# A hybrid decoder layer on one core: first head's logits one k tile later, its key sums seven k tiles apart, and the second chunk's first block loaded in the first down pair

## The chip, the cores and the metric

The kernel runs on 1 core of one Trainium2 chip. The metric is the device time of one execution in microseconds. The core has a matrix engine (TensorE, shown as PE, with its weight loads as PEld), a vector engine (DVE), a scalar engine (ACT), GpSimd (POOL), which here computes a little and issues DMAs, and SyncE (SP), which here only issues DMAs. All DMAs, whichever engine issues them, run on the core's 16 DMA engines.

## The reference

One decoder layer over 528 tokens (16 learned meta tokens and 512 tokens of input) with 2048 channels, all in float32:

```python
n = _rmsnorm(h, g_mix[l])
p = n @ w_in[l]                      # columns: q, k, v | b, c, u
o_attn = ...  # 8 heads of 128: z = q.k/sqrt(128) after RMS norm of q and k per head,
              # A[t,s] = sigmoid(z) * prod_{s<j<t} (1 - sigmoid(z_tj)), strictly causal
o_conv = gb * _causal_dwconv(gc * u, conv_w[l])          # 1024 channels, 3 taps
o = jnp.concatenate([_rmsnorm(o_attn, g_attn_out[l]), _rmsnorm(o_conv, g_conv_out[l])], axis=-1)
h = h + o @ w_out[l]
n2 = _rmsnorm(h, g_ffn[l])
h = h + (jax.nn.silu(n2 @ w_gate[l]) * (n2 @ w_up[l])) @ w_down[l]     # 5632 channels inside
```

The product over j is taken as a sum of logarithms over the keys behind s. The meta positions are dropped from the output.

## The kernel before

Everything is kept transposed: channels on the 128 partitions, tokens along the free axis. A float32 product is made of three matmuls: each operand is split into a high part (a cast to the matrix engine's fp32r type, on ACT) and a low part (the rest, a subtraction on DVE), and high x high, high x low and low x high are accumulated in PSUM. So each weight tile costs a DMA by SP into `w_buf` (L172), a cast on ACT into `s_buf` (L188) and a subtraction on DVE (L189). `split` (L293 to L295) does the same for activations.

The stages, in order of time:

- **Heads** (to about 338 us). For each of 8 heads the products k, q and v over 16 k tiles of 128 channels (`product`, L280 to L284, some 0.72 us a k tile). Attention work of a head is hung into the products of the next one: `after(n, work)` (L260) puts work on a list, and every k tile calls `tick` (L263), which runs what has come due. `attend` (L508) transposes v and makes the logits z (L527 to L533), `sums(2)`, `sums(1)`, `sums(0)` (L577) sum over the keys by matmuls with a triangle of ones into tiles c (L582 to L588), and `mix` (L607) makes the head's output o. For the first head, `attend` is due 11 k tiles after v, `sums(2)` 14 later, the other sums 6 apart and `mix` 11 later; for the others `attend` is due after 6.
- **Short convolution** (to about 595 us), two channel tiles by plain products, the other six by pairs of tiles, in `pair_product` (below).
- **Output projection** (to about 770 us). For each of 16 tiles i an attention half (`oa`) and a conv half (`oc`) of `wide_product` (L848 to L850) go into one PSUM tile `po` of two banks, `po[:, 0]` and `po[:, 1]`. For the last two tiles both attention halves come first, then both conv halves. DVE scales the halves in L907 and L931.
- **Gate and up** (to about 1610 us): 44 pairs f of `pair_product`, which makes a two by two block product of weights and activations with seven block products in place of eight. It has PSUM banks x, y, z; the order is block 0 into x, 1 into z, 2 onto x, 3 onto z, 4 onto x, 5 into y, 6 onto x (in the first pair of a weight matrix block 5 comes first). Between them ACT copies x and z aside (L769, L772, and after block 2 the copy u2, L775), and DVE makes c2 (L778 behind block 3, L783 behind block 4) and c1 (L788). `gate` (L1049) then makes silu(gate) * up; for odd f it makes five mixed blocks `odd` and `store_acts` splits them (L294 on ACT, 1280 wide, L295 on DVE) and stores them to DRAM tiles `fd` through POOL (L1043).
- **Down** (to the end). The 5632 channels are four chunks of 4, 6, 6 and 6 k tiles in pairs. For a chunk c the seven activation blocks (c, 0) to (c, 6) are loaded from `fd` by `load_acts` (L1067), two DMAs each on POOL (L1081). The first chunk has four pairs j of double width, which use `ring[0]` and the tiles `first1` to `first6`; the others have eight pairs each. Chunk 1 and later use twelve places of a ring in turn; block (1, 0) has place 6, block (1, 6) place 0. With `behind` given, POOL first makes a small write into the place (L1074) that reads a result of the pair before, which holds the load back until then. Results are scaled on DVE (L1121, L1127, L1128) and added to `out` by accumulating DMAs on POOL (L1113). The last pair adds on DVE instead and stores through SP (L1170 to L1177).

Memory places are taken from pools on two stacks; a new pool's tile waits for the last use of the tiles that lay there before. On the left stack, at the start of the down stage, `d` (8192 bytes a partition) and behind it ring place 6 (12544) come to lie where `f4` (16640) and the pool of `gu` (4864) lay.

The order of the instructions on each engine isn't that of the text: a planner simulates the program and picks, for each engine, the ready instruction with the best priority, which is the place in the text unless `tc.high_priority` raises it. `tc.stamp_issue_order_token(inst, name)` makes instructions of the same name keep the order of the text. Each engine, and POOL and SP as issuers of DMAs, then runs its instructions strictly in the order planned.

Of the kernel before, what the change touches and what calls it, by code (L numbers as in the profile page):

```python
# [12 lines left out]
ALU = mybir.AluOpType  # L13
# [9 lines left out]
KT = D // P  # L23
# [3 lines left out]
T2 = SEQ // 2  # L27
# [6 lines left out]
def hybrid_layer(ctx: ExitStack, tc: tile.TileContext, xT, w_in, w_out, w_gu, w_down, vecs, out):  # L34
# [148 lines left out]
    def split_quad(src, n, turn=False):  # L183
# [5 lines left out]
        in_turn(ve.tensor_tensor(lo, src, hi.bitcast(F32), ALU.subtract), turn)  # L189
        split_w.append((hi, lo, n))  # L190

    def in_turn(inst, on=True):
        if on:
            tc.stamp_issue_order_token(inst.ins, "first_pairs")
# [95 lines left out]
        for _ in product_steps(parts, acts, len(acts)):  # L290
            pass

    def split(hi, lo, src, eng=ve):  # L293
        sc.copy(hi, src)  # L294
        eng.tensor_tensor(lo, src, hi.bitcast(F32), ALU.subtract)  # L295

    def rsqrt(dst, v, n, y=None, t=None, eng=ve):
# [182 lines left out]
    def head(h):  # L480

        if h:
            pk = pp.tile([P, 2, 512], F32, tag="pp", name=f"pk{h}")
            product([(pk[:, 0, :H], 0, H), (pk[:, 1, :H], H, L)], n_hl)
        else:
            pk = pk0
        kn = kns[0]
        kh = apool.tile([P, 384], F32R, tag="kh", name=f"kh{h}")
        kl = apool.tile([P, 384], F32R, tag="kl", name=f"kl{h}")
        after(8 if h else 11, qk_norm(halves(pk, H), g_k, L, kn[:, :L], (kh, kl, 384), f"k{h}"))  # L490

        if h:
            pq = pp.tile([P, 2, 512], F32, tag="pp", name=f"pq{h}")
            product([(pq[:, 0, :], META, L)], n_hl)
        else:
            pq = pq0
        qn = apool.tile([P, SEQ], F32, tag="qn", name=f"qn{h}")
        qh = apool.tile([P, SEQ], F32R, tag="qh", name=f"qh{h}")
        ql = apool.tile([P, SEQ], F32R, tag="ql", name=f"ql{h}")
        after(9 if h else 12, qk_norm(pq[:, 0, :], gq_s, SEQ, qn, (qh, ql, SEQ), f"q{h}"))  # L500

        pv = pp.tile([P, 2, 512], F32, tag="pp", name=f"pv{h}")
        product([(pv[:, 0, :H], 0, H), (pv[:, 1, :H], H, L)], n_hl)
        vt = t512(L, "e", 2)
        ve.tensor_tensor(two(vt[:, :L]), halves(pv, H), two(r), ALU.mult)
        after(6 if h else 11, lambda: attend(h, kn, kh, kl, qn, qh, ql, vt))

    def attend(h, kn, kh, kl, qn, qh, ql, vt):  # L508

# [67 lines left out]
        def sums(s):  # L577
# [11 lines left out]
            if s:  # L589

                n, (a0, b0) = SEQ - Q0[s], SEG[s - 1]
                th, tl = hl[s - 1]
                ve.tensor_tensor(lw[0:1, b0 - n : b0], c[0:1, :n], sp[0:1, a : a + n], ALU.add)
                split(th[0:1, :], tl[0:1, :], lw[0:1, a0:b0])
                after(6, lambda: sums(s - 1))
            ve.tensor_tensor(lb[:, a:b], lb[:, a:b], c[:, : b - a], ALU.subtract)
            sc.activation(lw[:, a:b], lb[:, a:b], AF.Exp)
            causal(lw, s)
# [147 lines left out]
    def pair_product(acts, c1, c2, sides, m=1, fourth=None, second=None):  # L746
# [25 lines left out]
            sc.copy(p5, z)  # L772
        block_product(x, acts[2], False, m)
        with tc.high_priority(1 << 20):
            sc.copy(u2, x)  # L775
        block_product(z, acts[3], False, m)
        with tc.high_priority(1 << 20):
            in_turn(ve.scalar_tensor_tensor(c2[:, 0], z, -1.0, u2, ALU.mult, ALU.subtract), i == conv_pairs)  # L778
# [132 lines left out]
    for i, j in enumerate(OUT_TILES):  # L911
# [5 lines left out]
        if i < KT - 2:  # L917
            hj = attention_half(i, gp if half else ve)
        elif i == KT - 2:
            hs = [attention_half(m, ve) for m in (i, i + 1)]  # L920
        if i >= KT - 2:
            hj = hs[i - KT]
            run(wide_product(ps_out[i][:, 1, :], oc))
        ps = ps_out[i]
        t2 = wide_tmp("t2")
        if half == 1:

            src = hbuf.tile([P, 8, T2], F32, tag="src", name=f"src{k}")

        def residual(eng):  # L930
            ve.tensor_tensor(t2, ps[:, 1, :], acc_c, ALU.mult)  # L931
            eng.tensor_tensor(hj, hj, t2, ALU.add)
            sc.activation(src[:, 2 * half : 2 * half + 2], two(hj), AF.Copy, scale=g_ffn[:, j : j + 1])

# [98 lines left out]
    fd = [[dram.tile([P, 2, n, T2], F32R, name=f"fd{c}_{s}") for s in range(7)] for c, n in enumerate(CHUNKS)]  # L1033
    at = [(c, k) for c, n in enumerate(CHUNKS) for k in range(n)]

    def store_acts(blks, n, slots, kp):

        t = apool.tile([P, 2, n, T2], F32R, tag=f"s{n}", name=f"s{kp}_{n}")
        split(t[:, 0], t[:, 1], blks)
        c, k = at[kp]  # L1040
        for i, s in enumerate(slots):
            if kp < FT // 2 - 1:
                gp.dma_start(fd[c][s][:, :, k], t[:, :, i])  # L1043
            else:
                nc.sync.dma_start(fd[c][s][:, :, k].bitcast(F32), t[:, :, i].bitcast(F32))
# [3 lines left out]
    def gate(f, g1, u1, x):  # L1049
# [8 lines left out]
        else:  # L1058
# [3 lines left out]
            ve.tensor_tensor(odd[:, 2], odd[:, 1], even_f[:, 2], ALU.subtract)  # L1062
            ve.scalar_tensor_tensor(odd[:, 3], odd[:, 2], -1.0, even_f[:, 0], ALU.mult, ALU.subtract)
            ve.scalar_tensor_tensor(odd[:, 4], odd[:, 3], -1.0, odd[:, 0], ALU.mult, ALU.subtract)
            store_acts(odd, 5, (5, 6, 1, 2, 3), f // 2)

    def load_acts(c, s, behind=None):  # L1067

# [60 lines left out]
            add_down(j + n, c1[:, :, at])  # L1129

    for j in range(KT // 4):
        for s in ((0, 1), (2, 3), (4, 5))[j - 1] if j else ():
            load_acts(1, s, last)
        c1, c2 = (d, d2)[j % 2][:, 0:2], (d, d2)[j % 2][:, 2:4]
        last = c2[:, 0]
        x = pair_product(
# [11 lines left out]
    for c in range(1, len(CHUNKS)):  # L1148
        end = c == len(CHUNKS) - 1
        for j in range(KT // 2):  # L1150
# [18 lines left out]
            if last_pair:  # L1169
                ve.tensor_tensor(c2, c2, r_h, ALU.mult)  # L1170
                ve.tensor_tensor(c2, c2, h2[1], ALU.add)
                nc.sync.dma_start(two(out[2 * j + 1]), c2)
                ve.tensor_tensor(c1[:, 0], c1[:, 0], r_h[:, 0], ALU.mult)
                ve.tensor_tensor(c1[:, 0], c1[:, 0], h2[0][:, 0], ALU.add)
                ve.tensor_tensor(c1[:, 1], x, r_h[:, 1], ALU.mult)  # L1175
                ve.tensor_tensor(c1[:, 1], c1[:, 1], h2[0][:, 1], ALU.add)  # L1176
                nc.sync.dma_start(two(out[2 * j]), c1)  # L1177
            else:
                first_sums(2 * j, c1, x, 1)
    rings_p[2].release()  # L1180
# [61 lines left out]
```

## Time and profile before

| | us |
|---|---|
| median of 3 runs (lowest to highest) | 2040.29 (2039.11 to 2042.28) |
| the profiled execution's own time | 2040.52 |
| its span, first to last instruction | 2038.8 |
| PE busy | 2028.3 |
| DVE busy | 1721.0 |
| ACT busy | 1049.4 |
| POOL busy | 381.2 |

The span is that of one execution. Ends of matmuls are modelled, since matmuls are pipelined; the starts are measured, so the distance between starts tells what a matmul cost. In a row of a timeline stand the start, the length to the end of the last one, the engine, the line, the operation, what is written and read, and how many instructions the row holds; in brackets the engine's idle time ahead of it and who ended that.

### The profile page before, as it was taken

The numbers are of one execution on the slowest core, as the hardware profiler recorded it, in microseconds if no ns is written. First come the engines' busy times: TensorE is split into PE (matmuls) and PEld (weight loads), VectorE is DVE, ScalarE is ACT, GpSimd is POOL, SyncE is SP. The second block draws the span as 40 slices with busy tenths as digits, with TensorE's granted clock in tenths as the row PEclk, the third lists the DMA queues.
The fourth block names the chain that finished last, engine by engine and source line by source line (L and its number), as shares of the span: only waits on it lengthen the run. The fifth ranks groups of instructions, "written<-read, shape, count | busy, mean of one in ns | idle before, by whom it ended". The sixth has DMA issues, their size and how long they took to land.

```text
span 2038.8 us, 39740 instructions
## 1 busy us (share of the span) xinstructions
PE 2028.3 (99%) x16158; PEld 1966.2 (96%) x16158; DVE 1721.0 (84%) x2202; ACT 1049.4 (51%) x1517; POOL 381.2 (19%) x532
## 2 busy tenths in 40 slices
PE   9999999999999999999999999999999999999999
PEld 8999999999998889999999999999999999999999
DVE  8788878588977779989989989989989888888887
ACT  7666666344444436455555555555555544444443
POOL 0111111210015440111110110110110252222111
PEclk9999999999999999999999999999999999999999
DMA  6333344753366566555655654554655999989864
GB/s 231 113 117 125 125 137 130 254 146 104 104 219 184 177 189 224 166 163 169 169 162 149 170 164 146 171 161 150 167 161 151 289 305 292 247 236 260 231 152 89
DMA packets 161863, 361.70 MB, mean 177 GB/s; under 512 B 13584, under 2 KB 73488, under 8 KB 161680
## 3 DMA queue, kind: packets, MB, share of 16 engines
q1 hardware_dynamic: 79744, 229.51, 35.4%
q0 software_dynamic: 81936, 129.65, 24.3%
q8 instruction: 127, 2.08, 0.4%
q14 instruction: 56, 0.46, 0.1%
HBM read 278.50 MB, written 80.61 MB: 176 GB/s over the span
## 4 chain that ended last, share of the span: by engine, by line
PE 57%; DMA 1%; issue 1%; DVE 0%; POOL 0%; DVEq 0%; POOLq 0%
PE x L744 32%; PE z L744 16%; PE y L744 8%; DMA ring<-fd 1%; DMA out_T<-d 1%; DVE s_buf L189 0%; POOL out_T L1113 0%; POOL ring L1081 0%; POOL ring L1074 0%; DVE w_buf L201 0%; DVE d L783 0%; DVE d L1121 0%; DVE d L788 0%; DVE d L1175 0%; DVE d L1176 0%
## 5 line engine op out<-in xcount | busy, mean ns | idle before, releaser
L188 ACT CAST s_buf<-w_buf 128x1024 fp32r<-128x1024 f32 (+2 forms) x665 | 659.4, 992 | 759.4 <-PE x L744 369.8
L189 DVE TENSOR_TENSOR s_buf<-w_buf,s_buf 128x1024 fp32r<-128x1024 f32 (+2 forms) x665 | 766.9, 1153 | 127.8 <-ACT s_buf L188 121.5
L744 PE MATMUL x<-f,s_buf 128*128 128x256 f32 x4224 | 500.7, 275 | 0.6 <-ACT sides L775 0.5
L744 PEld LDWEIGHTS x<-f,s_buf 128*128 128x128 f32 x4224 | 488.9, 188 | 1.2 <-ACT sides L775 0.7
L201 DVE TENSOR_TENSOR w_buf<-w_buf 128x1024 f32<-128x1024 f32 (+1 forms) x243 | 278.3, 1145 | 17.2 <-DMA w_buf<-w_in 10.4
L744 PE MATMUL z<-f,s_buf 128*128 128x256 f32 x2112 | 253.6, 275 | 0.0
L744 PEld LDWEIGHTS z<-f,s_buf 128*128 128x128 f32 x2112 | 245.9, 188 | 0.0
L1043 POOL DMA_DIRECT2D fd<-s x147 | 103.6, 921 | 703.9 <-DVE s L295 702.6
L744 PE MATMUL x<-ring,s_buf 128*128 128x256 f32 x1824 | 219.9, 275 | 0.8 <-DMA ring<-fd 0.8
L744 PEld LDWEIGHTS x<-ring,s_buf 128*128 128x128 f32 x1824 | 213.1, 188 | 1.0 <-DMA ring<-fd 1.0
L744 PE MATMUL y<-f,s_buf 128*128 128x256 f32 x1056 | 126.8, 275 | 0.0
L744 PEld LDWEIGHTS y<-f,s_buf 128*128 128x128 f32 x1056 | 123.1, 188 | 0.1
L1113 POOL DMA_DIRECT2D out_T<-d x62 | 60.7, 1014 | 295.2 <-DVE d L1121 227.0
L744 PE MATMUL z<-ring,s_buf 128*128 128x256 f32 x864 | 105.7, 275 | 0.0
L744 PEld LDWEIGHTS z<-ring,s_buf 128*128 128x128 f32 x864 | 101.5, 188 | 0.0
L219 DVE TENSOR_TENSOR w_buf<-w_buf 128x1024 f32<-128x1024 f32 (+1 forms) x81 | 92.3, 1139 | 1.4 <-DMA w_buf<-w_down 1.4
L744 PE MATMUL x<-nh,s_buf 128*128 128x260 f32 x432 | 59.3, 282 | 0.0
L744 PE MATMUL y<-ring,s_buf 128*128 128x256 f32 x432 | 54.5, 279 | 2.2 <-DMA ring<-fd 2.2
L744 PEld LDWEIGHTS x<-nh,s_buf 128*128 128x128 f32 x432 | 55.0, 188 | 0.1
L744 PE MATMUL z<-blk,s_buf 128*128 128x260 f32 x432 | 54.8, 282 | 0.0
L744 PEld LDWEIGHTS y<-ring,s_buf 128*128 128x128 f32 x432 | 52.0, 192 | 2.6 <-issue 1.5
L778 DVE SCALAR_TENSOR_TENSOR gu<-z,sides 128x256 f32<-128x256 f32 x44 | 18.7, 425 | 42.4 <-PE z L744 40.6
(331 smaller groups left out, 3322.3 us busy)
## 6 DMA issues: line engine op xcount, KB each, us to landing
w_buf<-w_gu SPq DMA_DIRECT2D x176, 512.0 KB, 3.4
w_buf<-w_in SPq DMA_DIRECT2D x92, 512.0 KB, 3.4
fd<-s POOLq DMA_DIRECT2D x147, 256.0 KB, 5.3
w_buf<-w_down SPq DMA_DIRECT2D x96, 384.0 KB, 5.0
ring<-fd POOLq DMA_DIRECT2D x42, 768.0 KB, 10.0
w_buf<-w_out SPq DMA_DIRECT2D x32, 512.0 KB, 3.7
out_T<-d POOLq DMA_DIRECT2D x62, 256.0 KB, 5.6
fc<-st SPq DMA_DIRECT2D x8, 1040.0 KB, 6.1
```

Source lines behind the costliest of these rows:

```text
L188: sc.copy(hi, src)
L189: in_turn(ve.tensor_tensor(lo, src, hi.bitcast(F32), ALU.subtract), turn)
L201: in_turn(ve.tensor_tensor(sums[name], a, b, ALU.add), turn)
L219: ve.tensor_tensor(sums["t2"], sums["t2"], b["21"], ALU.add)
L744: pe.matmul(p, wt[:, kk], act(part, k), start=first, stop=wt is lo and k == n - 1, skip_group_check=skip)
L778: in_turn(ve.scalar_tensor_tensor(c2[:, 0], z, -1.0, u2, ALU.mult, ALU.subtract), i == conv_pairs)
L1043: gp.dma_start(fd[c][s][:, :, k], t[:, :, i])
L1113: gp.dma_start(two(out[j]), c, accum_op=ALU.add)
```

## The change

It has five parts.

1. In the first head, `attend` is due 12 k tiles after v in place of 11, and its sums are 7 k tiles apart in place of 6. The other heads are as before.
2. In the gate stage, the split and stores of f=1's mixed blocks are put on a list `late`, and run in the next pair (f=2), behind block 2 and its copy u2. An order token on that copy and on the split's cast keeps them in this order on ACT.
3. In the output projection, the conv halves of the last two tiles go into PSUM tiles of their own, `po_c14` and `po_c15`, from the pool `sm`.
4. In the first chunk of the down stage, the blocks of chunk 1 are loaded as 0 | 1, 2 | 3, 4 | 5 in pairs 0 to 3, in place of none | 0, 1 | 2, 3 | 4, 5. Pair 0's load has no `behind`. Block 6 is loaded in pair 3 as before.
5. In the last pair, the store of the last two half rows is split in two: the first half is stored as soon as it is done.

```diff
-    def split(hi, lo, src, eng=ve):
-        sc.copy(hi, src)
+    def split(hi, lo, src, eng=ve, turn=False):
+        in_order(sc.copy(hi, src), turn)
...
+    def in_order(inst, on):
+        if on:
+            tc.stamp_issue_order_token(inst.ins, "third_pair")
...
-        after(6 if h else 11, lambda: attend(h, kn, kh, kl, qn, qh, ql, vt))
+        after(6 if h else 12, lambda: attend(h, kn, kh, kl, qn, qh, ql, vt))
...
-                after(6, lambda: sums(s - 1))
+                after(6 if h else 7, lambda: sums(s - 1))
...
         with tc.high_priority(1 << 20):
-            sc.copy(u2, x)
+            in_order(sc.copy(u2, x), i == conv_pairs + 2)
+        if late:
+            late.pop()()
         block_product(z, acts[3], False, m)
...
+        conv_half = ps_out[i][:, 1, :]
         if i >= KT - 2:
-            hj = hs[i - KT]
-            run(wide_product(ps_out[i][:, 1, :], oc))
-        ps = ps_out[i]
+            hj, conv_half = hs[i - KT], small(f"po_c{i}")
+            run(wide_product(conv_half, oc))
...
-            ve.tensor_tensor(t2, ps[:, 1, :], acc_c, ALU.mult)
+            ve.tensor_tensor(t2, conv_half, acc_c, ALU.mult)
...
-            store_acts(odd, 5, (5, 6, 1, 2, 3), f // 2)
+            if f == 1:
+                late.append(lambda: store_acts(odd, 5, (5, 6, 1, 2, 3), 0, True))
+            else:
+                store_acts(odd, 5, (5, 6, 1, 2, 3), f // 2)
...
     for j in range(KT // 4):
-        for s in ((0, 1), (2, 3), (4, 5))[j - 1] if j else ():
-            load_acts(1, s, last)
+        for s in ((0,), (1, 2), (3, 4), (5,))[j]:
+            load_acts(1, s, last if j else None)
...
+                nc.sync.dma_start(out[2 * j][:, :T2], c1[:, 0])
                 ve.tensor_tensor(c1[:, 1], x, r_h[:, 1], ALU.mult)
                 ve.tensor_tensor(c1[:, 1], c1[:, 1], h2[0][:, 1], ALU.add)
-                nc.sync.dma_start(two(out[2 * j]), c1)
+                nc.sync.dma_start(out[2 * j][:, T2:], c1[:, 1])
```

More of the change, by code (lines that the diff above doesn't have):

```diff
@@ L190, in split_quad @@
         split_w.append((hi, lo, n))
+    late = []
+    def in_order(inst, on):
+        if on:
+            tc.stamp_issue_order_token(inst.ins, "third_pair")
     def in_turn(inst, on=True):
@@ L1034, in hybrid_layer, with store_acts @@
     at = [(c, k) for c, n in enumerate(CHUNKS) for k in range(n)]
-    def store_acts(blks, n, slots, kp):
+    def store_acts(blks, n, slots, kp, turn=False):
         t = apool.tile([P, 2, n, T2], F32R, tag=f"s{n}", name=f"s{kp}_{n}")
-        split(t[:, 0], t[:, 1], blks)
+        split(t[:, 0], t[:, 1], blks, turn=turn)
         c, k = at[kp]
```

## The prediction

> **What bounds the kernel now.** I read the page first, then the list of what TensorE waits for, then the timeline of PE alone, looking for places where the distance between two matmuls is longer than their usual one.
>
> ```profile
> span 2038.8 us, 39740 instructions
> PE 2028.3 (99%) x16158; PEld 1966.2 (96%) x16158; DVE 1721.0 (84%) x2202; ACT 1049.4 (51%) x1517; POOL 381.2 (19%) x532
> ```
>
> TensorE is busy all the time but 10.5 us, and the change adds or removes no matmul. So it can win only what PE loses in holes and in slowed matmuls. The profiled execution took 2040.52 us, that is 1.72 around its span; the median of the runs shown is 2040.29, 0.23 lower. Sums are made against 2040.52. About 0.2% of this, 4.1 us, is what a measurement of this kernel can tell from no change.
>
> The large hole lies where the down product goes from its first chunk to its second. Timeline of PE there, and two pieces of the chain of waits (the first of undisturbed matmuls); columns are start and length in us:
>
> ```profile
> 1694.71 0.84 PE L744 MATMUL x<-ring,s_buf 128*128 128x256 f32 x6
> 1696.35 1.68 PE L744 MATMUL x<-ring,s_buf 128*128 128x256 f32 x12 [0.79 <-DMA ring<-fd]
> 1699.33 0.94 PE L744 MATMUL y<-ring,s_buf 128*128 128x256 f32 x6 [1.30 <-DMA ring<-fd]
> 1701.19 2.91 PE L744 MATMUL y<-ring,s_buf 128*128 128x256 f32 x12 [0.92 <-DMA ring<-fd]
> 1703.90 4.65 PE L744 MATMUL x<-ring,s_buf 128*128 128x256 f32 x36
> 1708.39 0.84 PE L744 MATMUL z<-ring,s_buf 128*128 128x256 f32 x6
> ```
> ```profile
> 1718.75 4.08 PE x L744 x36
> 1683.19 17.96 DMA ring<-fd
> 1670.50 12.40 DMA out_T<-d
> ```
>
> Undisturbed, 36 matmuls take 4.08 us, 0.113 each. The 72 from 1694.71 to 1708.39 took 13.68 instead of 8.16: **5.52 us lost**. Three waits start it: the second part of block 4 lands at 1696.3, the two parts of block 5 at 1699.3 and 1701.15. The rest is the clock: the 12 matmuls from 1701.19 take 2.71 instead of 1.36, the 36 after them 4.49 instead of 4.08, 1.76 us together, and the granted clock of this stretch is 0.83 (third column from the end of the first row):
>
> ```profile
> 1694.70:1704.80 10.10, 7.08 (x43) 6.51 (x42) 5.87 (x9) 2.08 (x3) 2.63 (x4) 0.83 1.17 312
> 1625.00:1630.00 5.00, 5.00 (x47) 5.00 (x45) 5.00 (x7) 2.11 (x2) 0.00 (x0) 1.00 1.00 332
> 1630.00:1635.00 5.00, 5.00 (x47) 5.00 (x46) 5.00 (x6) 2.33 (x3) 1.90 (x2) 1.00 0.49 134
> 1650.00:1660.00 10.00, 10.00 (x90) 10.00 (x90) 8.10 (x12) 5.69 (x7) 8.42 (x10) 1.00 1.14 364
> ```
>
> The last two columns are the DMA engines' share and GB/s. The loads are late because the transfers are one saturated train from about 1636 on (1.14 and more), while 1630 to 1635 is half empty.
>
> **Part 1: the second chunk's first block in the first down pair.** Before, pairs 1, 2, 3 load blocks 0-1, 2-3, 4-5, and pair 3 also block 6; after, pairs 0 to 3 load 0, 1-2, 3-4, 5, and 6. The bytes are the same; one block (two parts of 768 KB, 1.57 MB) leaves the train at its head. POOL, which issues them, and the DVE instruction that last reads what lies under block 0's place:
>
> ```profile
> 1608.14 1.43 POOL L1081 DMA_DIRECT2D first<-fd  x2 [3.76 <-PE y L744]
> 1633.10 1.14 POOL L1113 DMA_DIRECT2D out_T<-d  x1 [23.53 <-DVE d L1121]
> 1669.79 0.72 POOL L1081 DMA_DIRECT2D ring<-fd  x1 [8.68 <-PE x L744]
> 1675.34 1.33 POOL L1081 DMA_DIRECT2D ring<-fd  x1
> 1676.72 2.57 POOL L1081 DMA_DIRECT2D ring<-fd  x2
> 1683.19 0.71 POOL L1081 DMA_DIRECT2D ring<-fd  x1 [2.12 <-DMA out_T<-d]
> ```
> ```profile
> 1616.29 0.69 DVE L1061 TENSOR_TENSOR odd<-gu,gu 128x512 f32<-128x512 f32 x1
> ```
>
> By the sizes in the code, block 0's place (12544 bytes behind d's 8192) lies within f4 and gu. f4 is read by PE long before; gu last by the row of L1061, until 1616.98. So the two new issues go out at about 1617, in POOL's pause of 23.53 us; nothing on POOL stands behind them until 1633.10. No L1074 touch is needed for this block, one of POOL's in pair 3 goes. On their queue they stand behind the first chunk's loads, so they don't take those loads' turn. Room: against 364 GB/s, 1625 to 1630 has 32 left and 1630 to 1635 has 230, 1.3 MB of the 1.57; some 0.3 MB (0.7 us) runs into the train.
>
> What that does at the end: 1669.79 and 1675.34 wait for PE and are block 6; 1676.72 (x2) is block 4, and two later issues, of which 1683.19 is the last, are block 5. With one block fewer ahead, block 5 takes block 4's turn: both parts there by 1696.35 at the latest plus the 0.7. It is needed, with PE not held, at 1694.71 + 18 x 0.113 = 1696.75 (part one, which has the earlier landing) and 1697.43 (part two). Block 4 takes block 3's turn, and PE never waited for that. **Slack 0.4 us**, so I book 5.2 of the 5.52, bounds 5.5 (all) and 3.5 (block 5 is 2 us late, no slowed clock). If the slack is gone, block 5 is what is late next. All of it moves with PE: issues follow DVE's sums, which follow PE.
>
> **Part 2: the third pair's ACT.** In gate pair f=2, PE's block 4 overwrites x, whose copy (L775) must be done first:
>
> ```profile
> 817.67 2.88 PE L744 MATMUL z<-f,s_buf 128*128 128x256 f32 x24
> 821.04 3.02 PE L744 MATMUL x<-f,s_buf 128*128 128x256 f32 x24 [0.49 <-ACT sides L775]
> 823.90 2.88 PE L744 MATMUL y<-f,s_buf 128*128 128x256 f32 x24
> 826.90 5.73 PE L744 MATMUL x<-f,s_buf 128*128 128x256 f32 x48
> ```
> ```profile
> 818.50 1.27 ACT L294 CAST s<-odd 128x1280 fp32r<-128x1280 f32 x1 [2.94 <-DVE odd L1064]
> 820.63 0.36 ACT L775 COPY sides<-x 128x256 f32<-128x256 f32 x1
> ```
> ```profile
> 819.80 1.49 DVE L295 TENSOR_TENSOR s<-odd,s 128x1280 fp32r<-128x1280 f32 x1 [1.33 <-ACT s L294]
> 826.34 0.42 DVE L783 SCALAR_TENSOR_TENSOR gu<-x,sides 128x256 f32<-128x256 f32 x1
> ```
>
> 24 matmuls take 2.72, so PE lost 0.65 before 821.04, 0.14 behind it and 0.28 before 826.90 (there it waits for L783): 1.07 us. x is ready at about 818.0, but ACT stands for 2.94 us at f=1's split, which waits for odd. The change puts that split behind the copy, so the copy runs in this pause and 0.79 is won. The split itself (1.27 on ACT, 1.49 on DVE, then five stores on POOL) is only moved; ACT has its pause as cover, DVE its 1.33 us idle. Without that cover L783 would be 1.49 later, at PE's cost. DVE is full here, PE arrives 0.79 earlier at L783's reader, and DVE gains about 1.1 to 1.3 from the pause: that gap stays near 0.2. Booked **0.9**; bounds 1.1 and -0.7 (0.79 less 1.49).
>
> **Part 3: own PSUM tile for the last two conv halves.**
>
> ```profile
> 758.92 0.68 DVE L907 TENSOR_TENSOR w<-po,acc_a 128x512 f32<-128x512 f32 x1
> ```
> ```profile
> 759.03 0.39 PE L850 MATMUL po<-oa,s_buf 128*128 128x512 f32 x1
> 759.75 0.47 PE L848 MATMUL po<-oc,s_buf 128*128 128x512 f32 x1 [0.34 <-ACT st L294]
> ```
>
> Matmuls of this width come every 0.23, so 0.49 is lost. The row names ACT, but L907, which reads the attention half of the very tile whose conv half PE is to write, ends at 759.60, 0.15 before PE goes on. A tile of its own ends that: **0.5** won; bounds 0.5 and 0. Against this speaks the Trainium skill, "PSUM — Partial Sum Buffer", section "Summary: rules for kernel authors": an engine may read while a matmul runs if the matmul targets a different bank. The two halves are such, so by that rule L907 held nothing, ACT did, and the gain would be 0; the 0.15 us decides for me.
>
> **Part 4: first head.** Its logits come one k tile (about 0.72 us) later, its later sums a k tile further apart.
>
> ```profile
> 55.50 0.40 PE L284 MATMUL pk<-nh,s_buf 128*128 128x264 f32 x2
> 56.05 0.80 PE L527 MATMUL z<-qh,kh 128*128 128x512 f32 x3
> 75.24 0.40 PE L282 MATMUL pv<-nl,s_buf 128*128 128x264 f32 x2
> 75.97 0.50 PE L588 MATMUL c<-spl,carry 128*128 128x512 f32 x1 [0.33 <-DVE spl L295]
> ```
>
> Two matmuls take 0.24, so 0.31 is lost before z and 0.49 before c. A k tile covers either, but the planner sets a new order on PE, DVE and ACT, and the first head's last product then stands three k tiles ahead of the second head's logits, not six. Booked **0.6** of 0.8; bounds 0.9 and -1.0 (each of the two stalls moved once more and 0.1 larger).
>
> **Part 5: last store in two.**
>
> ```profile
> 2035.45 0.43 DVE L1176 TENSOR_TENSOR d<-d,h 128x256 f32<-128x256 f32 x1
> ```
> ```profile
> vec<-vecs SPq DMA_DIRECT2D x1, 37.5 KB, 1.8
> out_T<-d SPq DMA_DIRECT2D x2, 256.0 KB, 2.3
> ```
>
> What remains behind the last DVE result is 128 KB instead of 256. By the rows it lands in 1.8 to 2.3: between 0.5 won and nothing; a loss of 0.3, should it queue behind its first half, is the other bound. Booked **0.1**. The first half's issue stands on an SP that has nothing else to do.
>
> **Sum.** 5.2 + 0.9 + 0.5 + 0.6 + 0.1 = 7.3; 2040.5 - 7.3 = 2033.2.
>
> **Rivals.**
> *Train still late* (0.17). Block 0's transfer, or the weights and stores it displaces between 1617 and 1636, push the train by 2 us rather than 0.7. For it: 0.4 us of slack is thin. Against: 134 GB/s of traffic in the half-empty stretch. PE then waits 1 to 1.5 and may pay the 1.76 of slow clock: 2034.5 to 2036.3, say 2035.4. The Trainium skill, "TensorE: Matmul & The Clock Gate", section "What's actually happening", lets the clock fall only after an idle window of some 3.4 us, so by it this wait costs itself alone; here waits of 0.79, 1.30 and 0.92 were followed by 0.83, so I keep the slow clock in.
>
> *The early stalls only move* (0.10). DVE is full around the third pair, and the first head's order is the planner's. Parts 2 and 4 give nothing: 2040.5 - 5.8 = 2034.7; as much against as for.
>
> *The block isn't loaded earlier* (0.08): the planner puts its issue behind the sums at 1633.10. Three blocks then follow in pair 1, block 5 lands at 1701.15 as now, and only block 4's wait (0.96) goes: 2040.5 - 0.96 - 2.1 = 2037.4. Against it: its place is free at 1617 and POOL idle.
>
> *Slower: POOL blocked* (0.05). POOL runs in order. If block 0's place comes free late, the issue holds up the sums and touches behind it, and with them blocks 1 to 6. Every us behind 1633.10 moves the train by one. It decides from about 1640 on: 7 us late makes block 5 land at 1703.4, a wait of 6.0 plus 1.76 against the 2.1 won elsewhere and the 5.52 that stood there before. At 1645 it is 2045.5. Against it: what lies under the place.
>
> **Numbers.** Forecast 2033.2 with 0.60, its own range 2031.8 to 2034.6. Low end: all bounds' gains, 5.5 + 1.1 + 0.5 + 0.9 + 0.5 = 8.5, 2032.0, less some run-to-run spread: 2031.2. High end: the unloaded block, 2037.4. Faster by over 0.2% means below 2036.2: forecast, moved stalls and most of the late train, 0.82; within 0.2%: the unloaded block and the rest, 0.13; slower 0.05.
>
> **What would show it.** Part 1: ring loads on POOL near 1617, DMA share near 1 from 1630 to 1635, no wait of PE on ring<-fd, clock 1.00 across the switch. A wait of x or z there instead of y would say that another block is last. Part 2: L775 ahead of L294, and no gap before block 4; a larger one before the last x would be DVE. Part 3: po_c follows po at 0.23 us. Part 4: no gap of over 0.2 before z or c of the first head. I am wrong if PE still waits over 1 us at the switch, or if new gaps of a us show in heads 0 and 1.

## The result, and the profile after

| | before | after |
|---|---|---|
| median of 7 runs each, us (lowest to highest) | 2041.68 (2039.11 to 2043.32) | 2034.83 (2033.74 to 2035.37) |
| ratio of after to before, 95% interval | | 0.9969 (0.9958 to 0.9980) |
| the profiled execution's own time | 2040.52 | 2033.74 |
| its span | 2038.8 | 2031.9 |

The kernel became 6.85 us faster by the medians, 0.34% (0.31% by the ratio); forecast were 7.3 us from the profiled execution of the kernel before, 2033.2. Line numbers of the kernel after are higher: L744 is now L750, L1081 L1092, L1113 L1124, L294 L300, L775 L781, L783 L791, L907 L915.

The page of after, its first rows:

```profile
span 2031.9 us, 39737 instructions
PE 2025.8 (100%) x16158; PEld 1964.4 (97%) x16158; DVE 1721.0 (85%) x2202; ACT 1050.5 (52%) x1517; POOL 381.5 (19%) x531
```

What TensorE waits for in it (total, times, longest, in us):

```profile
PE warm L85 <- DVE one L81: 1.1, 1, 1.1
PE c L593 <- ACT sph L300: 0.3, 1, 0.3
...
PE c L594 <- DVE spl L301: 0.2, 1, 0.2
PE z L533 <- ACT qh L300: 0.2, 1, 0.2
```

The waits on `ring<-fd`, on the copy and on `st` are gone; z still waits. Where each part acted is read from the starts of the same matmuls in the two traces. The number is after minus before, so a step down is a gain:

| place | before | after | difference |
|---|---|---|---|
| first head's v begins | 29.77 | 29.84 | +0.07 |
| third head's v begins | 113.87 | 113.78 | -0.09 |
| last head's v begins | 323.16 | 323.33 | +0.17 |
| gate stage begins | 770.71 | 770.37 | -0.34 |
| third gate pair, last x | 826.90 | 825.49 | -1.41 |
| last undisturbed block ahead of the switch | 1694.71 | 1693.17 | -1.54 |
| first undisturbed block behind it | 1708.39 | 1701.33 | -7.06 |
| end of the span | 2038.8 | 2031.9 | -6.9 |

**The switch.** Timeline of PE in after:

```profile
1693.17 2.20 PE L750 MATMUL x<-ring,s_buf 128*128 128x256 f32 x18
1695.21 2.20 PE L750 MATMUL y<-ring,s_buf 128*128 128x256 f32 x18
1697.25 4.24 PE L750 MATMUL x<-ring,s_buf 128*128 128x256 f32 x36
1701.33 2.20 PE L750 MATMUL z<-ring,s_buf 128*128 128x256 f32 x18
```

The 72 matmuls from 1693.17 to 1701.33 take 8.16 us, which is 72 x 0.113: nothing of the 5.52 us is left. POOL's issues, and the stretches of the transfers (the last three columns are granted clock, DMA share and GB/s):

```profile
1615.05 1.43 POOL L1092 DMA_DIRECT2D ring<-fd  x2 [7.02 <-DVE odd L1069]
...
1675.02 2.59 POOL L1092 DMA_DIRECT2D ring<-fd  x2
```
```profile
1694.70:1704.80 10.10, 10.10 (x91) 10.10 (x91) 9.11 (x14) 4.73 (x7) 3.94 (x5) 1.00 1.09 271
1620.00:1625.00 5.00, 5.00 (x47) 5.00 (x46) 4.97 (x7) 1.68 (x3) 0.00 (x0) 1.00 1.19 391
1625.00:1630.00 5.00, 5.00 (x46) 5.00 (x46) 5.00 (x6) 1.68 (x3) 0.00 (x0) 1.00 1.08 388
1630.00:1635.00 5.00, 5.00 (x46) 5.00 (x46) 5.00 (x8) 3.02 (x4) 3.94 (x5) 1.00 1.01 261
```

Block 0 goes out at 1615.05, as soon as L1069 has read what lay there, in POOL's pause. The half-empty stretch from 1630 to 1635 now moves 261 GB/s in place of 134. Block 5's two parts, the issues of 1675.02, land by the trace at 1690.8 and 1693.55; they are needed at 1695.21 and six matmuls later, 1695.9.

From issue to landing the second part still takes 17.8 us (from 1675.76), before it took 18.0 (1683.19 to 1701.15). So what moved is the issue: it goes out 7.4 us earlier, 1.5 of them with PE as a whole. In the old order POOL stood for 2.12 us ahead of that issue until an earlier transfer had landed (the row of 1683.19 in the prediction); in after and in e1, below, it stands for none. In the traces of e2, e3, e11 and e12, below, the same hold is there, 1.6 to 2.8 us long.

**The third gate pair.** Timelines of PE, ACT and DVE in after:

```profile
817.33 2.88 PE L750 MATMUL z<-f,s_buf 128*128 128x256 f32 x24
820.05 2.88 PE L750 MATMUL x<-f,s_buf 128*128 128x256 f32 x24
...
825.49 5.60 PE L750 MATMUL x<-f,s_buf 128*128 128x256 f32 x48
```
```profile
817.58 0.36 ACT L781 COPY sides<-x 128x256 f32<-128x256 f32 x1
818.16 1.27 ACT L300 CAST s<-odd 128x1280 fp32r<-128x1280 f32 x1 [0.21 <-DVE odd L1072]
```
```profile
822.46 1.23 DVE L207 TENSOR_TENSOR w_buf<-w_buf 128x1024 f32<-128x1024 f32 x1
823.60 0.42 DVE L791 SCALAR_TENSOR_TENSOR gu<-x,sides 128x256 f32<-128x256 f32 x1
```

The copy now runs ahead of the split. From block 3 (817.33) to the last x (825.49) are 8.16 us in place of 9.23: 1.07 won, and another 0.1 in the matmuls behind. L791 stands behind one weight sum, and the next L207 follows it at 825.07; before, its counterpart L783 came behind two, at 826.34, and PE waited for it. DVE ahead of that, before:

```profile
823.93 2.49 DVE L201 TENSOR_TENSOR w_buf<-w_buf 128x1024 f32<-128x1024 f32 x2
```

**The conv halves.** Timelines of PE, DVE and ACT in after, and last the cast that PE's row of before named, in before:

```profile
759.26 0.39 PE L858 MATMUL po<-oa,s_buf 128*128 128x512 f32 x1
759.49 0.39 PE L856 MATMUL po_c<-oc,s_buf 128*128 128x512 f32 x1
```
```profile
759.16 0.68 DVE L915 TENSOR_TENSOR w<-po,acc_a 128x512 f32<-128x512 f32 x1
```
```profile
759.27 0.62 ACT L300 CAST st<-src 128x512 fp32r<-128x512 f32 x1 [3.20 <-DVE src L952]
```
```profile
759.04 0.62 ACT L294 CAST st<-src 128x512 fp32r<-128x512 f32 x1 [3.21 <-DVE src L944]
```

`po_c` follows at 0.23 us, while both L915 and the cast of `st` still run, to 759.84 and 759.89. PE needed neither.

**The first head.** Timelines of PE and DVE in after:

```profile
56.06 0.81 PE L533 MATMUL z<-qh,kh 128*128 128x512 f32 x3 [0.19 <-ACT qh L300]
...
77.55 0.50 PE L594 MATMUL c<-spl,carry 128*128 128x512 f32 x1
```
```profile
54.22 0.54 DVE L301 TENSOR_TENSOR vl<-va,vh 128x384 fp32r<-128x384 f32 x1
54.69 0.67 DVE L478 TENSOR_TENSOR qn<-tmp,tmp 128x512 f32<-128x512 f32 x1
```

z begins at 56.06, before at 56.05. The values' transposes moved a k tile back, but qn did not come earlier (54.67 before), since the value copies still stand ahead of it, and the planner put z among the last matmuls of the same product. What PE loses there is 0.35 in place of 0.31. The gap before the last c shrank from 0.49 to 0.16.

### The profile page after: what moved, and what is told of

Same layout as the page of the kernel before. It is cut to its first block, busy times and chain, and to the rows that moved or that the text cites. A ratio compares the mean times of both kernels' runs of the same rounds, so it can differ in the third digit from the quotient of the medians.

```text
span 2031.9 us, 39737 instructions
## 1 busy us (share of the span) xinstructions
PE 2025.8 (100%) x16158; PEld 1964.4 (97%) x16158; DVE 1721.0 (85%) x2202; ACT 1050.5 (52%) x1517; POOL 381.5 (19%) x531
## 4 chain that ended last, share of the span: by engine, by line
PE 97%; DVE 2%; ACT 1%; issue 0%; POOL 0%; DVEq 0%; ACTq 0%
PE x L750 40%; PE z L750 20%; PE y L750 10%; PE po L857 3%; PE po L856 3%; PE po L858 3%; PE pv L286 2%; PE pv L288 1%; PE pv L290 1%; PE pq L290 1%; PE pq L286 1%; PE pq L288 1%; PE pk L286 1%; PE pk L288 1%; PE pk L290 1%; PE pcu L288 0%
## 5 line engine op out<-in xcount | busy, mean ns | idle before, releaser
L750 PE MATMUL x<-f,s_buf 128*128 128x256 f32 x4224 | 500.4, 275 | 0.0
L750 PEld LDWEIGHTS x<-f,s_buf 128*128 128x128 f32 x4224 | 488.8, 188 | 0.2
L207 DVE TENSOR_TENSOR w_buf<-w_buf 128x1024 f32<-128x1024 f32 (+1 forms) x243 | 278.3, 1145 | 17.4 <-DMA w_buf<-w_in 10.7
L750 PE MATMUL z<-f,s_buf 128*128 128x256 f32 x2112 | 253.6, 275 | 0.0
L750 PEld LDWEIGHTS z<-f,s_buf 128*128 128x128 f32 x2112 | 245.9, 188 | 0.0
L750 PE MATMUL x<-ring,s_buf 128*128 128x256 f32 x1824 | 219.2, 275 | 0.0
L750 PEld LDWEIGHTS x<-ring,s_buf 128*128 128x128 f32 x1824 | 212.4, 188 | 0.0
L750 PE MATMUL y<-f,s_buf 128*128 128x256 f32 x1056 | 126.8, 275 | 0.0
L750 PEld LDWEIGHTS y<-f,s_buf 128*128 128x128 f32 x1056 | 123.1, 188 | 0.1
L1124 POOL DMA_DIRECT2D out_T<-d x62 | 60.7, 1014 | 285.5 <-DVE d L1132 221.8
L750 PE MATMUL z<-ring,s_buf 128*128 128x256 f32 x864 | 105.7, 275 | 0.0
L750 PEld LDWEIGHTS z<-ring,s_buf 128*128 128x128 f32 x864 | 101.5, 188 | 0.0
L225 DVE TENSOR_TENSOR w_buf<-w_buf 128x1024 f32<-128x1024 f32 (+1 forms) x81 | 92.3, 1139 | 0.7 <-DMA w_buf<-w_down 0.7
L750 PE MATMUL x<-nh,s_buf 128*128 128x260 f32 x432 | 59.3, 282 | 0.0
L750 PEld LDWEIGHTS x<-nh,s_buf 128*128 128x128 f32 x432 | 55.0, 188 | 0.1
L750 PE MATMUL z<-blk,s_buf 128*128 128x260 f32 x432 | 54.8, 282 | 0.0
L286 PE MATMUL pv<-nh,s_buf 128*128 128x264 f32 x256 | 53.1, 288 | 0.2 <-ACT tmp L464 0.2
L750 PEld LDWEIGHTS z<-blk,s_buf 128*128 128x128 f32 x432 | 53.1, 188 | 0.0
```

What stands on the lines that cost most here:

```text
L207: in_turn(ve.tensor_tensor(sums[name], a, b, ALU.add), turn)
L225: ve.tensor_tensor(sums["t2"], sums["t2"], b["21"], ALU.add)
L286: pe.matmul(ps, wh, ah[:, a:b], start=k == 0, stop=False)
L750: pe.matmul(p, wt[:, kk], act(part, k), start=first, stop=wt is lo and k == n - 1, skip_group_check=skip)
```

## Experiments

Differences of PE's starts are read as in the table above. e1 to e4 ran on one chip, e5 to e8 on a second, e9 and e10 on a third, e11 and e12 on a fourth, each beside the kernel before. The kernel after ran beside it only in the first comparison and in e5. The parts are numbered as in the prediction: 1 load order, 2 the third pair's ACT, 3 own PSUM tile, 4 first head, 5 last store.

### The load order alone, and everything but it

```diff
 # e1_p1_only: kernel before, with
-        for s in ((0, 1), (2, 3), (4, 5))[j - 1] if j else ():
-            load_acts(1, s, last)
+        for s in ((0,), (1, 2), (3, 4), (5,))[j]:
+            load_acts(1, s, last if j else None)
 # e2_no_p1: kernel after, with the reverse
```

> The kernel before with one edit of the change: the second chunk's blocks are loaded 0 | 1-2 | 3-4 | 5 over the four down pairs. Theory A (block 5 takes block 4's turn in the transfers, so the waits at the switch and the slowed matmuls behind them go): 5.2 to 5.6 us faster than before, the granted clock 1.00 from 1690 to 1705, no wait of PE on ring<-fd. Rival (train still late): PE still waits on ring<-fd at the switch, 2 to 4 us faster only. Rival (the gain of the whole change came mostly from the earlier stages): under 2 us faster.

> The changed kernel with the old order of loads (0-1, 2-3, 4-5 in pairs 1 to 3). Theory A: it loses 5.2 to 5.6 us against the changed kernel and so stands 1.2 to 1.7 us under the kernel before, with the waits of block 4's second part and of block 5 and a granted clock of about 0.83 at the switch. If parts 2 to 4 shift the transfers too (they bring DVE's sums, and with them the issues, 1.5 us earlier), the waits stay the same, since needs and issues move together. Rival (parts of the change depend on each other): more than 3 us under before, or not under it.

On this chip the kernel before took 2040.34 us (median of 31 runs). The load order alone took 2036.53 (ratio 0.9981, 0.9971 to 0.9991), 3.8 us less; everything but it 2038.18 (0.9993, 0.9984 to 1.0003), 2.2 less. By the starts of its matmuls the first gained 5.5 us between 1696 and 1706 (from +1.6 against before to -3.9) with no wait on `ring<-fd`; the +1.6 it brought along from the start of the program and the heads, where its program is that of before. In its list of waits the stalls of parts 2 and 3 stand as before:

```profile
PE x L744 <- ACT sides L775: 0.5, 1, 0.5
PE po L848 <- ACT st L294: 0.3, 1, 0.3
```

Without the load order, PE's timeline at the switch is broken again:

```profile
1693.23 2.54 PE L750 MATMUL x<-ring,s_buf 128*128 128x256 f32 x18
1696.87 0.95 PE L750 MATMUL y<-ring,s_buf 128*128 128x256 f32 x6 [1.11 <-DMA ring<-fd]
1698.97 2.93 PE L750 MATMUL y<-ring,s_buf 128*128 128x256 f32 x12 [1.15 <-DMA ring<-fd]
...
1706.04 2.20 PE L750 MATMUL z<-ring,s_buf 128*128 128x256 f32 x18
```

1693.23 to 1706.04 are 12.81 us for 72 matmuls of 0.113: 4.65 lost. That is less than the 5.2 to 5.6 expected, and the kernel stands 2.2 under before in place of 1.2 to 1.7. The load order removes the waits, by itself, and the other four parts are worth about 2. That the gain of e1 is 5.5 in the trace and 3.8 in the medians led to the runs of the kernel before, below.

### Block 0 in the second pair

```diff
-        for s in ((0,), (1, 2), (3, 4), (5,))[j]:
+        for s in ((), (0, 1, 2), (3, 4), (5,))[j]:
```

> The changed kernel with block 0 loaded in the second down pair, together with blocks 1 and 2; blocks 3-4 and 5 stay where the change puts them. It tells whether the early place of block 0 in time or the new grouping of the later blocks brings the gain. Theory A (the transfers are one saturated train, and what counts is that 1.57 MB go ahead of its start): block 5 lands 3 to 5 us later than in the changed kernel, at 1697 to 1699 against a need at 1695.2 and 1695.9, so PE waits 1.5 to 3 us and pays up to 1.8 us of slow clock: 2 to 5 us slower than the changed kernel. Rival (grouping alone): within 0.5 us of the changed kernel, no wait on ring<-fd.

2037.77 us (0.9993, 0.9984 to 1.0003). PE in the trace:

```profile
1692.80 2.20 PE L750 MATMUL x<-ring,s_buf 128*128 128x256 f32 x18
1696.56 0.95 PE L750 MATMUL y<-ring,s_buf 128*128 128x256 f32 x6 [1.56 <-DMA ring<-fd]
1698.55 1.66 PE L750 MATMUL y<-ring,s_buf 128*128 128x256 f32 x12 [1.04 <-DMA ring<-fd]
1700.05 4.24 PE L750 MATMUL x<-ring,s_buf 128*128 128x256 f32 x36
```

Block 5 lands at 1696.4 and 1698.5, and 3.2 us are lost (1692.80 to the block after the last row, 1704.13, less 8.16). So the early place of block 0 in time is needed; the new grouping of the others alone does not do it. Whether the grouping brings part of the gain (3.2 lost here, 4.65 in e2), one execution each doesn't tell. In this execution the clock did not slow down (1.00); its ten times reach from 2035.83 to 2043.81, and those of 2040 and more have mean granted clocks of 0.998 or 0.999, the others mostly 1.0.

### Two blocks in the first pair

```diff
-        for s in ((0,), (1, 2), (3, 4), (5,))[j]:
+        for s in ((0, 1), (2, 3), (4, 5), ())[j]:
```

> The changed kernel with blocks 0 and 1 of the second chunk in the first down pair, 2-3 in the second, 4-5 in the third. Block 1's place lies under what the last act stores are sent from (they land at about 1631.5), so its issue on POOL should wait for that, with the sums of the first pair behind it. Theory (such a wait costs nothing before about 1640): both blocks are there by 1640, block 5 lands 5 us or more before its need, no wait on ring<-fd, within 0.5 us of the changed kernel. Rival (POOL blocked): the sums and touches behind the issue are late, PE waits at the switch or in the first pairs, 2 us or more slower.

2034.45 us, beside 2034.49 for the kernel after on that chip. POOL's issue of block 1 stood behind that of block 0 and went out at 1634.02, with the first pair's sums behind it, some 3 us later than in after, measured against PE. The trace names DVE's L225 as what released it, not the stores that were expected. No wait on `ring<-fd` followed, and by the trace block 5 landed at 1681.3, 15 us ahead of its need. So POOL held up to 1634 costs nothing, as the rival "POOL blocked" had it. Its price from 1640 on was not reached by any run.

### The first head's old distances, and a longer one

```diff
 # e4_no_p4: kernel after, with
-        after(6 if h else 12, lambda: attend(...))
+        after(6 if h else 11, lambda: attend(...))
-                after(6 if h else 7, lambda: sums(s - 1))
+                after(6, lambda: sums(s - 1))
 # e8_attend13: kernel after, with
-        after(6 if h else 12, lambda: attend(...))
+        after(6 if h else 13, lambda: attend(...))
```

> The changed kernel with the first head's old distances (11 products ahead of its logits, 6 between its sums). Theory (part 4 gave nothing: in the traces PE stands 0.22 us earlier after the first head, the gap before z stays 0.3 because qn and qh still queue behind the value copies on DVE, the sums' gap of 0.49 shrinks to 0.16, and the new order costs 0.3 to 0.4 us in heads 2 to 8): the PE ledger shows the gap of 0.49 before the last c again and the drift of heads 2 to 8 gone; within 0.5 us of the changed kernel, 0.2 us faster as the likeliest. Rival (part 4 did bring its 0.6, and the drift in heads 2 to 8 has another cause, parts 1 to 3): 0.6 us slower than the changed kernel, the drift still there.

> The changed kernel with the first head's logits 13 products after its values instead of 12. In the changed kernel PE stands for 0.35 us before z, because DVE makes qn only after two value copies and qh follows qn; one k tile more did not help. Theory (the planner puts z where its own model has qh ready, and the distance only decides what stands ahead of qn on DVE): with 13 the values' copies fall behind qn, qn is 0.6 to 0.8 us earlier, z too, and a gap of 0.2 to 0.4 us stays before z. Rival (one more k tile covers it): z at the same time or later, the gap under 0.1 us.

Without part 4 the time is 2034.85 (0.9976, 0.9966 to 0.9985). A gain of tenths is read better from the stage: from the first head's v to the third's takes 84.08 to 84.17 us in the five profiled executions with the old distances (before, e1, e4, e11, e12) and 83.87 to 83.94 in the eight with the new ones (after, e2, e3, e5, e6, e7, e9, e10). So part 4 gives 0.2. The gap of 0.49 before the last c is there again in e4, as expected, but for the rest both expectations were wrong: I had taken the 0.3 to 0.4 that after drifts back in heads 3 to 8 for the price of the new order. But from the third to the last head's v it takes 209.1 to 209.9 us with the new order and 209.3 to 210.2 with the old, from one execution to the next, so this is scatter.

With 13 the stage takes 84.57, 0.65 more (the one run took 2034.99 us). PE there:

```profile
56.08 0.81 PE L533 MATMUL z<-qh,kh 128*128 128x512 f32 x3 [0.39 <-DVE v L524]
...
88.46 0.50 PE L619 MATMUL o<-wl,vh 128*128 128x512 f32 x1 [0.58 <-DVE wl L301]
```

The value copies fell behind qn on DVE, and qn and z came 0.4 us earlier relative to the start of the head, less than the 0.6 to 0.8 expected. The planner moved z five matmuls ahead within the product, and the gap before it grew to 0.56, now put down to the value copy; a new one of 0.75 came before o. A longer distance does not cover this wait; the order on DVE and the planner's own place for z set it.

### The third pair's split at its old place

```diff
-            in_order(sc.copy(u2, x), i == conv_pairs + 2)
+            in_order(sc.copy(u2, x), False)
-            if f == 1:
+            if f == -1:
```

> The changed kernel with f=1's split and its stores back at their old place, ahead of the third pair's copy. Theory (all of the 1.14 us that PE gained between 815 and 828 comes from this step: 0.79 before block 4 and the rest because DVE makes L791 ahead of its two weight sums instead of behind them): the gaps of 0.5 and 0.3 us are back, PE 1.0 to 1.2 us later from 828 on, 1.1 us slower than the changed kernel. Rival (only the copy's 0.8 comes from it, the rest from the stages before): 0.7 to 0.8 us later.

2035.69 us (0.9979, 0.9970 to 0.9988; the kernel before 2040.13 on that chip). Against after, PE is 0.21 later at block 3 (817.54), 1.29 at the last x (826.78) and 1.41 from the next block on (832.34), and its row of block 4 is that of before:

```profile
820.91 3.02 PE L750 MATMUL x<-f,s_buf 128*128 128x256 f32 x24 [0.49 <-ACT sides L781]
```

So 1.1 to 1.2 us are lost here, all that after had won. On DVE the two weight sums L207 stand ahead of L791 again, together: the planner's order there follows the place of the split.

### The kernel after again, and the last head's distance

```diff
 # e5_after_again: the kernel after
 # e6_last_head: kernel after, with
-                after(6 if h else 7, lambda: sums(s - 1))
+                after(7 if h in (0, HEADS - 1) else 6, lambda: sums(s - 1))
 # e10_best: e6_last_head, and the last store in one piece
-                nc.sync.dma_start(out[2 * j][:, :T2], c1[:, 0])
-                nc.sync.dma_start(out[2 * j][:, T2:], c1[:, 1])
+                nc.sync.dma_start(two(out[2 * j]), c1)
```

> The changed kernel once more, beside the others. Theory (the profiled execution of the kernel before holds a slowed clock at the switch that only some of its executions have): the changed kernel, which never waits there, has a granted clock of 1.0 in all executions, and its median stands 5.0 to 6.0 us under that of the kernel before, less than the 6.85 of the first comparison. Rival (the ledger of the two profiled executions is the true difference): 6.5 to 7.5 us under it.

> The changed kernel with the distance of seven k tiles between the sums for the last head too, whose sums stand among the first conv products (two gaps of 0.42 and 0.49 us before L593 and L594 at 364.5 in the changed kernel). Theory (there a k tile more covers both, as it took 0.34 of 0.49 before the last sum of the first head): PE 0.7 to 0.9 us earlier from 366 on, 0.7 us faster than the changed kernel. Rival (the planner moves the gap along, as with the logits of the first head): 0 to 0.3 us.

> The changed kernel with seven k tiles between the last head's sums and the last store in one piece again. Theory: PE 0.9 us earlier at 366 as in the run of that edit alone; the 1.2 us that its profiled execution lost at 431 (DVE's weight sum L207 stood 1.83 us for a late weight tile, ahead of L786 and L791) was a matter of that execution and is not there again; the end of the program comes 4.14 to 4.17 us after PE's last start instead of 4.25: 0.8 to 1.0 us faster than the changed kernel, 6.5 to 7.5 us under the kernel before. Rival (PE 0.9 us earlier runs into the weight tiles' transfers each time): the wait at 431 is there again, within 0.4 us of the changed kernel.

The kernel after took 2034.49 on another chip, 6.45 us under before's 2040.94 there (0.9968, 0.9956 to 0.9981), between the two expectations; its mean granted clock was 1.0 in all five runs. With the last head's distance the time is 2033.65 (0.9962, 0.9949 to 0.9974), and with the last store in one piece as well 2034.19 on a third chip, 5.94 under before (0.9969, 0.9957 to 0.9981). By the medians e6 is 0.84 us faster than after on its chip, near the 0.7 expected; e10 misses its 6.5 to 7.5. In the traces of both the gain is lost again; e6:

```profile
429.64 1.23 DVE L207 TENSOR_TENSOR w_buf<-w_buf 128x1024 f32<-128x1024 f32 x1 [1.83 <-DMA w_buf<-w_in]
430.78 0.42 DVE L786 SCALAR_TENSOR_TENSOR tmp<-z,sides_c 128x260 f32<-128x260 f32 x1
```
```profile
432.73 1.23 PE L750 MATMUL x<-nh,s_buf 128*128 128x260 f32 x8 [1.25 <-DVE tmp L791]
```

Against after, PE won 0.98 us at 366, and lost 1.35 at 431: a weight tile issued at 422.19 needed 7.35 us to land (5.21 and 6.14 in the two traces of after), DVE's weight sum stood for it, and the two results that PE needs stood behind that sum. In e10's trace the same wait is there, 1.17 us, so it was no matter of one execution, as I had expected. But both traces are of the slowest of their kernel's executions (2034.26 of 2031.88 to 2034.26, 2035.06 of 2032.78 to 2035.06), so the others need not have this wait. Whether e6 is faster than after, five runs of each don't settle, and why the tile lands later isn't shown.

The last store in one piece ends the program 4.16 us after PE's last start, as expected. All profiled executions with it in one piece lie at 4.14 to 4.17, all with it in two at 4.25 to 4.27.

### The kernel before, twice more

```diff
 # e11_before_again, e12_before_third: the kernel before
```

> The kernel before once more, for a second profiled execution. Theory (what is lost at the switch differs from one execution to the next: the waits on block 5 are always there, the slowed clock behind them only in the executions whose mean granted clock is 0.999 or less): where the mean clock is 1.0, the granted clock stays at 1.00 from 1690 to 1706 and 3 to 4 us are lost there instead of 5.5; where it is 0.999, some 5 to 6. Rival (the loss of 5.5 us is there in every execution, and part 1 is worth it always): 5.2 us or more, the clock at 0.8 to 0.9.

> The kernel before a third time, for the same question: 3 to 4 us lost at the switch with the clock at 1.00 there, or 5 to 6 with a slowed clock, by the theory; always 5.2 or more by the rival.

The single runs took 2042.51 us (e11, mean granted clock 0.998) and 2041.60 (e12, 1.0); a third execution of the kernel beside them took 2042.62 (1.0). Their stretch of the switch, from 1694.70, and PE there; first e11, then e12:

```profile
1694.70:1704.80 10.10, 7.22 (x44) 6.56 (x43) 6.25 (x9) 2.01 (x3) 3.34 (x5) 0.77 1.16 327
```
```profile
1695.72 2.61 PE L744 MATMUL x<-ring,s_buf 128*128 128x256 f32 x18
1700.56 1.62 PE L744 MATMUL y<-ring,s_buf 128*128 128x256 f32 x6 [2.23 <-DMA ring<-fd]
...
1710.35 2.20 PE L744 MATMUL z<-ring,s_buf 128*128 128x256 f32 x18
```
```profile
1694.70:1704.80 10.10, 6.37 (x49) 5.63 (x48) 6.86 (x10) 2.01 (x4) 3.05 (x5) 1.00 1.16 336
```
```profile
1694.37 2.20 PE L744 MATMUL z<-ring,s_buf 128*128 128x256 f32 x18
...
1698.64 1.66 PE L744 MATMUL x<-ring,s_buf 128*128 128x256 f32 x12 [1.05 <-DMA ring<-fd]
1701.50 0.94 PE L744 MATMUL y<-ring,s_buf 128*128 128x256 f32 x6 [1.20 <-DMA ring<-fd]
1703.85 1.67 PE L744 MATMUL y<-ring,s_buf 128*128 128x256 f32 x12 [1.41 <-DMA ring<-fd]
1705.37 4.24 PE L744 MATMUL x<-ring,s_buf 128*128 128x256 f32 x36
```

In e11 1695.72 to 1710.35 are 14.63 us for 72 matmuls, 6.5 lost; in e12 1694.37 to 1705.37 are 11.0 for 54, 4.9 lost. So the loss does differ from one execution to the next, and the slowed clock is there in two of three profiled executions. But e12 lost 4.9 without it, because its waits were longer (3.66 us against 2.79 in e11): my 3 to 4 was too low, and the rival's 5.2 too high.

## Why the prediction was right, and where it was off

**Part 1** (booked 5.2, measured 5.5). The mechanism held in every point named: the issues in POOL's pause (1615.05 for "about 1617"), the half-empty stretch filled (0.49 to 1.01), no wait on `ring<-fd`, clock 1.00. Only the slack was mis-sized: 2.3 us in place of 0.4. The step that failed is "some 0.3 MB runs into the train": I counted the room from 1625 on, but the issue is earlier, and there was room from 1620 on too, as before's row shows beside the 391 GB/s of after:

```profile
1620.00:1625.00 5.00, 5.00 (x46) 5.00 (x45) 4.97 (x5) 3.10 (x4) 0.00 (x0) 1.00 1.02 313
```

From 1620 to 1635 after moves 5 x (78 + 56 + 127), 1.3 MB more than before. Beside e2, which stands at the same time as after and differs from it by the load order alone (356, 209 and 164 GB/s in these stretches), it is 5 x (35 + 179 + 97), 1.56 MB: the whole block of 1.57, whose two parts landed at 1625.3 and 1628.0. So nothing ran into the train, which gives back the 0.7 that was to spill; the other 1.2 us of slack is not accounted for. Nor did the train stand at "1.14 and more" from 1636 on: in before the share is 1.02 from 1635 to 1640 and 1.12 from 1640 to 1650. The rival "train still late" needed that spill; e3 shows what it would have cost, 3.2 us and sometimes more. "The block isn't loaded earlier" is out by 1615.05, and "POOL blocked" by e7 at least up to 1634. The sum was made against one execution that lost 5.52 at the switch; with e11, e12 and e2, executions with the old load order lose 4.65 to 6.5 there, so the true gain of this part is a spread. The medians of e1 (3.8, with an interval of about 2 either way) do not contradict it, but those of e2 and e4, 3.3 apart with part 4 as the other difference, are low too: over many executions the part may be worth nearer 3.5 to 4 than 5.5, and these runs don't settle it.

**Part 2** (booked 0.9, measured 1.1 to 1.2, bound 1.1). The copy went ahead as worked out. The size that was off is the gap ahead of L783, forecast to stay "near 0.2": the planner put its counterpart ahead of the second weight sum, and the gap vanished; e9 shows that this hangs on the same edit.

**Part 3** (booked 0.5, measured 0.49). It was not ACT that PE waited for: in after ACT's cast ends at 759.89, 0.4 behind the matmul that the row of before put it ahead of, and e1, without this part, has the old wait. That leaves L907. The 0.15 us that decided for me was a thin reason, since in before ACT's cast ended at 759.66, nearer still to PE's 759.75; that L907 reads the very tile was the better one. The two halves lie in different banks, and yet PE stood for the reader of the other one; by the rule of the Trainium skill, "PSUM — Partial Sum Buffer", section "Summary: rules for kernel authors", there was nothing to gain. That rule says what may run side by side; the wait here was most likely one that the program itself set, on the tile as a whole. No run takes out this part alone or shows that dependency by itself.

**Part 4** (booked 0.6, measured 0.2). "A k tile covers either" is the step that failed. For c it covered 0.34 of 0.49. For z it covered nothing: the wait is not a distance on PE but qn's place in DVE's queue, and the planner places z by its own reckoning of when qh is there. The feared new stalls of a us in the first two heads did not come.

**Part 5** (booked 0.1, measured -0.1). The last 128 KB landed in 1.70 us in place of 2.02 for 256 KB, inside the bounds, but the end of the program came 0.1 later after PE's last start, in each of the profiled executions. The step that failed: I took the landing for the end. From the landing to the end it takes 0.9 with one piece and 1.33 with two; what takes the time there isn't shown.

**The sum.** 5.5 + 1.15 + 0.5 + 0.2 - 0.1 is 7.25, and 7.3 was forecast; the errors of parts 1 and 2 (+0.55) and of parts 4 and 5 (-0.6) cancelled, so that the total came so near is luck. The two profiled spans differ by 6.9, since the heads of after took 0.3 more by scatter. The medians differ by 6.85, and by 6.45 on the second chip. Against the median the forecast of 2033.2 is 1.6 us low: 2034.83 lies 0.2 above the range that went with the 0.60, and within the outer one. The time alone would fit two rivals as well, "the early stalls only move" (2034.7) and "train still late" (2034.5 to 2036.3); what decides against them are the traces, in which no wait is left at the switch and parts 2 and 3 gained in their own places. The rival "the early stalls only move" was true of half of part 4 and of nothing else.

## What to carry to other kernels

A late transfer at the end of a saturated train is mended at the train's head: look for the last stretch that is not full, for an issuer that is idle in it and a place that is free by then, and count the room of that stretch from the moment of the issue. Before a stall is covered by distance, see what stands ahead of the late operand on its own engine, since a planner that believes the operand in time moves the reader along. And a gain that brings an engine forward can run into a transfer that was just in time (0.98 won, 1.35 lost in one execution): look at what is next due behind the place, not only at the place.

## What the runs showed of the hardware

- The slowed clock does not follow the sum of the waits. Matmuls with waits of 1.05, 1.20 and 1.41 us between them (e12), or 1.56 and 1.04 (e3), kept a granted clock of 1.00; 0.79, 1.30 and 0.92 (before), 1.11 and 1.15 (e2: 0.83 over the same stretch), or 2.23 and 0.56 (e11: 0.77) did not. The Trainium skill, "TensorE: Matmul & The Clock Gate", section "What's actually happening", lets the clock fall only behind an idle window of some 3.4 us, and no single wait here is as long. What decides stays open. Where the clock falls, matmuls take twice as long: the 12 behind the last wait 2.71 us in before and 2.73 in e2 and e11, in place of 1.36.
- The mean granted clock goes with the time, but does not tell the longer executions apart. Of 31 runs of the kernel before on one chip, 17 have 1.0 and a median of 2039.75 us, and 14 have 0.998 or 0.999 and a median of 2041.0. But on two other chips executions with 1.0 took 2042.41 and 2042.62. The kernel after has 1.0 in all 12 runs.
- Three executions of the kernel before differ by 0.7 us in the first 30 us alone (29.77 to 30.47 at the first head's v), and by 0.8 us over heads 3 to 8 (209.3 to 210.1); with the other kernels, whose text is the same up to there and in those heads, it is up to 1.4 (to 31.19) and 0.9 us. Gains of a few tenths can be told only within their own stage.
